# Gated delta-net on one core: the work behind each convolution is laid down 24 contraction tiles later, in steps of even period, with the output gates on their own and GpSimd taking scaling, masks and copies

## The chip, the core and the metric

One core of one Trainium2 chip runs the whole program. Its engines work side by side, each in the fixed order of its own queue: TensorE (PE in the profile, with its weight loads as PEld), VectorE (DVE), ScalarE (ACT), GpSimd (POOL) and the queue SP, which here issues the DMAs. The metric is the device time of one execution in microseconds; lower is better.

## What is computed

One inference step of a two-layer decoder trunk: a prompt of 512 tokens and 8 decoding sequences of 4 tokens each, 544 columns in all, width 1024. Layer 0 mixes tokens with an mLSTM, layer 1 with a gated delta-net; each is followed by a squared-ReLU MLP and layer norms. The change is in layer 1's mixer alone. Cut from the reference:

```python
proj = x @ w_in
qkv, z = proj[..., :CONV_DIM], proj[..., CONV_DIM:CONV_DIM + VW_B]
c = sum(xp[:, j:j + T] * conv_w[j] for j in range(4))      # xp: 3 old rows, then qkv
c = silu(c); new_conv = xp[:, T:]
q = l2norm(c[q part]) * DK_B ** -0.5; k = l2norm(c[k part]); v = c[v part]
# per head, in chunks: A = strictly lower part of (beta k) k^T * decay, plus I
u, w = triangular_solve(A, [beta v, beta k exp(G)])
for each chunk:
    v_new = u - w S
    o     = (q exp(G)) S + (q k^T * decay) v_new
    S     = exp(G_last) S + (k exp(G_last - G))^T v_new
o = head_rms(o) * norm_w * silu(z)
return o @ w_out, S, new_conv
```

There are 8 key heads and 16 value heads of 128 by 128. The prompt has one state per head, and each of the 8 decoding sequences has its own, which is read, used and written back.

## The kernel before

All large products are made of float32 values split into a high and a low part (`split`, L111 and L112: a copy on ACT, a subtraction on DVE), with three products for each contraction tile of 128: `mm3` (L194) issues them, 272 columns at a time, and calls `tick()` after each contraction tile. A "contraction tile" below is one such call, three matmuls. Weights come in blocks of 128 by 1024, by DMA into `wraw`, then split into `wh` (ACT) and `wl` (DVE).

Layer 1's mixer works on 8 units; a unit is one key head with its two value heads. The string `ORDER` sets the sequence of the large products: `p0` to `p7` project a unit (`project`: key, query and two values, 16 contraction tiles each), `y0` to `y3` project the output gates of a pair of units and apply them (`gate_out`), `w0` to `w3` multiply a pair with the output weights (`out`). Behind each of a unit's four projections stands `conv`: ACT copies the projection from PSUM into a padded buffer `pre`, ACT and DVE make the four-tap convolution `acc` (L996, L998), a sigmoid is made by a clamp on DVE (L510) and three ACT passes (L511 to L513), and DVE multiplies (L1002). Right behind it the code puts the transposes and norms that need its result (L1040, L1049, L1065).

The rest of a unit is cut into steps by `yield`, and three lanes run such steps: `lane_i` (`prepare` builds the decayed products and inverts 16 by 16 blocks on DVE, L1128 and L1130, sending them through DRAM, `dx`, back to `xc`; `invert` builds the full inverse with small matmuls L1167 to L1214), `lane_s` (`scan`: the chunk loop L1257, L1268, L1275, L1284, L1246), and `lane_d` (`decode` and `update` for the 8 sequences: L1371, L1422, and on DVE the masks L1414 and the states L1427). Every `tick()` counts a lane down, and at zero, every `period` contraction tiles, the lane runs its next step. `PERIODS` sets the periods for the lanes i, s and d: 3, 3, 4 from p0, 5, 5, 6 from y0, 3, 3, 6 from p7. Where a result must be there, `finish(...)` runs the steps of all lanes, one after another, with no contraction tile between them: in `gate_out` for the units of its pair, and before p3 to p7 for a unit whose buffers are wanted again. The inversion of eight units and these calls are the places that the prediction speaks of.

The place of an instruction in the code is its priority; when the program is built, each engine's queue is laid down in the order in which work is taken to be ready, so that neighbours in the code can change places. On the chip each queue is then worked off in that order, and an instruction that waits holds all behind it.

## Time and profile before

| | us |
|---|---|
| median of 3 runs | 1814.6 (1813.19 to 1815.72) |
| the profiled execution | 1814.86 |
| its span, first to last instruction | 1813.2 |
| TensorE busy | 1742.2 |
| VectorE busy | 1062.3 |
| ScalarE busy | 831.2 |
| GpSimd busy | 56.1 |
| the delta-net's stretch, from 705 to 1420 us of the span | 715 |

The span is the stretch that the rows below cover; the 1.7 us between it and the profiled execution's own time lie around it and stay as they are. "PEclk" in a row is the granted clock of TensorE as a share of 2.4 GHz; it has two levels, 1.0 (2.4 GHz) and 0.5 (1.2 GHz), and a value between them is a mean over the stretch.

### The profile page before, as it was taken

To read this page: it belongs to the slowest core of one execution; us is meant where nothing else is said; L and a number is where in the kernel's file an instruction comes from. 1 tells how busy PE (TensorE), PEld (TensorE's weight loads), DVE (VectorE), ACT (ScalarE), POOL (GpSimd) and SP (SyncE) were. 2 spreads that over 40 slices of the span, in tenths; PEclk is the share of its full clock that TensorE was granted. 3 is DMA by queue.
4 is the path that set the end of the run, shared out by engine and by line. 5 is a ranking of instruction groups with operands and counts; after the bars stand their busy time and mean duration, and the time that the engine had idled before them with its cause. 6 is when DMAs were issued, how large, how long until landed. Compare 5 with 4: busy or idle time off the path is not lost.

```text
span 1813.2 us, 35720 instructions
## 1 busy us (share of the span) xinstructions
PE 1742.2 (96%) x14580; PEld 1678.0 (93%) x14580; DVE 1062.3 (59%) x2648; ACT 831.2 (46%) x1874; POOL 56.1 (3%) x105
## 2 busy tenths in 40 slices
PE   7999999999999999899979999999898999999997
PEld 7999998999999999899869989998898999999996
DVE  6564767432244368777856877785488543234436
ACT  6444346331244137775644764575246542134314
POOL 2000000000000000011001000000000000000000
PEclk9999999999999999899979999997799999999998
DMA  4131232222223221223324323421242222222311
GB/s 161 59 106 62 70 97 93 71 94 82 94 82 117 82 75 62 56 58 102 104 64 143 105 66 104 141 80 39 78 132 73 94 85 91 90 86 93 106 59 50
DMA packets 84293, 158.89 MB, mean 88 GB/s; under 512 B 37536, under 2 KB 41504, under 8 KB 83616
## 3 DMA queue, kind: packets, MB, share of 16 engines
q1 hardware_dynamic: 84128, 156.60, 27.6%
q8 instruction: 115, 1.88, 0.4%
q14 instruction: 50, 0.41, 0.1%
HBM read 140.51 MB, written 16.06 MB: 86 GB/s over the span
## 4 chain that ended last, share of the span: by engine, by line
PE 80%; DVE 10%; ACT 4%; DMA 3%; issue 1%; POOL 1%; SPq 0%; ACTq 0%; DVEq 0%; POOLq 0%
PE pg_t L194 39%; PE pm_s L194 13%; PE pm_a L194 12%; PE pm_s L1371 2%; DVE lnt L380 1%; PE pm_s L1422 1%; DVE lnt L381 1%; PE pm_s L1257 1%; DMA xc<-dx 1%; PE pm_s L1268 1%; PE pm_a L1093 1%; DVE wl L112 1%; DVE acc L998 1%; PE pm_s L1275 1%; DVE XL L392 1%
## 5 line engine op out<-in xcount | busy, mean ns | idle before, releaser
L112 DVE TENSOR_TENSOR wl<-wraw,wh 128x1024 fp32r<-128x1024 f32 x200 | 245.3, 1227 | 370.6 <-ACT wh L111 369.8
L194 PE MATMUL pg_t<-XH,wh 128*128 128x272 f32 x1480 | 443.9, 300 | 3.3 <-ACT wh L111 2.8
L194 PE MATMUL pg_t<-XH,wl 128*128 128x272 f32 x1480 | 437.6, 296 | 1.0 <-DVE wl L112 1.0
L194 PE MATMUL pg_t<-XL,wh 128*128 128x272 f32 x1480 | 438.3, 296 | 0.0
L111 ACT CAST wh<-wraw 128x1024 fp32r<-128x1024 f32 (+1 forms) x201 | 210.1, 1045 | 472.7 <-PE pg_t L194 221.2
L194 PEld LDWEIGHTS pg_t<-XH,wh 128*128 128x128 f32 x1480 | 284.6, 192 | 7.4 <-ACT wh L111 4.5
L194 PEld LDWEIGHTS pg_t<-XH,wl 128*128 128x128 f32 x1480 | 283.8, 192 | 3.1 <-DVE wl L112 1.7
L194 PEld LDWEIGHTS pg_t<-XL,wh 128*128 128x128 f32 x1480 | 284.4, 192 | 2.0
L194 PE MATMUL pg_t<-h,wh 128*128 128x272 f32 x672 | 129.2, 289 | 0.0
L194 PEld LDWEIGHTS pg_t<-h,wh 128*128 128x128 f32 x672 | 105.8, 189 | 0.3
L194 PE MATMUL pg_t<-h,wl 128*128 128x272 f32 x336 | 97.0, 289 | 0.0
L194 PE MATMUL pm_a<-h,wh 128*128 128x272 f32 x496 | 95.3, 289 | 0.0
L194 PE MATMUL pm_s<-h,wh 128*128 128x272 f32 x496 | 95.0, 289 | 0.0
L194 PE MATMUL pm_s<-XH,wh 128*128 128x272 f32 x288 | 84.7, 294 | 0.0
L194 PE MATMUL pm_s<-XL,wh 128*128 128x272 f32 x288 | 84.4, 293 | 0.0
L194 PE MATMUL pm_s<-XH,wl 128*128 128x272 f32 x288 | 84.3, 293 | 0.0
L194 PE MATMUL pm_a<-XL,wh 128*128 128x272 f32 x280 | 82.3, 294 | 0.8 <-DVE XL L392 0.8
L396 DVE SCALAR_TENSOR_TENSOR XR<-XR,pg_t 128x272 f32<-128x272 f32 x118 | 51.0, 434 | 54.4 <-PE pg_t L194 53.9
L194 PE MATMUL pm_a<-XH,wh 128*128 128x272 f32 x280 | 82.6, 295 | 0.0
L194 PE MATMUL pm_a<-XH,wl 128*128 128x272 f32 x280 | 81.3, 290 | 0.0
L194 PEld LDWEIGHTS pm_s<-h,wh 128*128 128x128 f32 x496 | 78.0, 189 | 0.2
L194 PEld LDWEIGHTS pm_a<-h,wh 128*128 128x128 f32 x496 | 78.0, 188 | 0.1
(573 smaller groups left out, 3910.8 us busy)
## 6 DMA issues: line engine op xcount, KB each, us to landing
wraw<-in_w SPq DMA_DIRECT2D x64, 512.0 KB, 3.5
wraw<-in_wb SPq DMA_DIRECT2D x48, 512.0 KB, 3.5
wraw<-in_w2a SPq DMA_DIRECT2D x32, 512.0 KB, 3.5
sst<-in_s SPq DMA_DIRECT2D x64, 256.0 KB, 3.1
wraw<-in_wa SPq DMA_DIRECT2D x24, 512.0 KB, 3.5
wraw<-in_w2b SPq DMA_DIRECT2D x24, 512.0 KB, 3.5
wraw<-in_wbo SPq DMA_DIRECT2D x16, 512.0 KB, 3.7
out_ss<-sst SPq DMA_DIRECT2D x32, 256.0 KB, 2.7
```

The lines of the kernel that those rows point to most:

```text
L111: S.copy(hi, src)
L112: V.tensor_tensor(lo, src, r32(hi), op=ALU.subtract)
L194: T.matmul(ps, lhsT=wt[:, k, :], rhs=xt[k][:, HS[h]], start=first and k == 0 and q == 0, stop=last and k == n - 1 and q == 2,)
L380: V.tensor_tensor(t, x, rs, op=ALU.mult)
L381: V.tensor_tensor(t, t, mu, op=ALU.subtract)
L392: V.tensor_tensor(XL[j][:, HS[h]], x, r32(XH[j][:, HS[h]]), op=ALU.subtract)
L396: V.scalar_tensor_tensor(x, x, ALPHA if first else 1.0, ps, op0=ALU.mult, op1=ALU.add)
L998: V.scalar_tensor_tensor(acc, pre[:, q:q + WC], cw[q], acc, op0=ALU.mult, op1=ALU.add)
L1093: T.matmul(pk[:, q * 256:(q + 1) * 256], lhsT=kq[:, 0, c0:c0 + P], rhs=kq[:, :, c0:c0 + P], start=True, stop=True)
L1257: T.matmul(pks[:, w], lhsT=kq[:, w, cc], rhs=St, start=True, stop=True)
L1268: T.matmul(pv[:, j], lhsT=X[:, 4 * (ch // 2) + 2 * j + ch % 2], rhs=rhs[:, j] if ch else vtok[:, j, 0], start=True, stop=True)
L1371: T.matmul(pkq[:, r], lhsT=t[:, r], rhs=kqf[:, :, o:o + 4], start=True, stop=True)
```

## The change

- `ORDER` runs `g` in place of `y`, earlier: g0 follows p2, g1 follows p4, g2 follows p6, g3 stands between w2 and w3. `gate(g)` projects and makes the gates alone and keeps them in four `yh` buffers; `gated(u)`, a new step, multiplies them with a unit's outputs and splits the product. It runs in a fourth lane, `lane_m`.
- `finish` moves from the gates to the front of each `w`: w0 waits for `m1`, w1 for `m3`, w2 for `m5`, w3 for `m7`.
- `PERIODS` for i, s, d and m is 6, 5, 6, 4 from p0 on, and 4, 4, 6, 3 from w2 on.
- The transposes and norms behind a convolution become the functions `keys`, `queries` and `values`, put on the list `later`; `tick()` runs them 24 contraction tiles after (`LAG`). A unit's inversion then waits for its `q`, its scan for its `v`.
- In `prepare` the recursion on 16 by 16 blocks is one step, no longer five, and after the DMA of `xc` three empty steps follow (`REST`).
- GpSimd takes from DVE: in `conv` the clearing of `pre`, the copy of the old rows into it and the two copies to `cvo`; the copy in `kqx`; in `update` the masks `VM` (8 operations of 128 columns for 2 of 512), and the scaling of the states by their decay (4 of 128 columns). DVE's four multiply-adds of 128 columns for four states become one addition of 512 columns. `update` has three empty steps ahead of the first head of each half.
- The two products for the decoding tokens in `conv` become one.

The core of the diff:

```diff
-ORDER = "p0 p1 p2 p3 y0 w0 p4 p5 y1 w1 p6 p7 y2 w2 y3 w3"
-PERIODS = {"p0": (3, 3, 4), "y0": (5, 5, 6), "p7": (3, 3, 6)}
+ORDER = "p0 p1 p2 g0 p3 w0 p4 g1 p5 w1 p6 g2 p7 w2 g3 w3"
+PERIODS = {"p0": (6, 5, 6, 4), "w2": (4, 4, 6, 3)}
+LAG = 24
+REST = 3
...
+    def run_later():
+        key, work = later.pop(0)[1:]
+        work()
+        done.add(key)
 
     def tick():
+        now[0] += 1
+        while later and later[0][0] <= now[0]:
+            run_later()
         for lane in lanes:
             lane.tick()
...
-            V.memset(pre[:, 0:3], 0.0)
-            V.tensor_copy(samp(pre)[:, :, 0:3], cvt[:, slot])
+            G.memset(pre[:, 0:3], 0.0)
+            G.tensor_copy(samp(pre)[:, :, 0:3], cvt[:, slot])
...
-            V.tensor_copy(cvo[:, 0:3], pre[:, TP:TP + 3])
-            V.tensor_copy(cvo[:, 3:27].rearrange("p (b t) -> p b t", t=3), samp(pre)[:, :, 4:7])
+            G.tensor_copy(cvo[:, 0:3], pre[:, TP:TP + 3])
+            G.tensor_copy(cvo[:, 3:27].rearrange("p (b t) -> p b t", t=3), samp(pre)[:, :, 4:7])
...
+                later.append((now[0] + LAG, f"{'kq'[w]}{u}", (keys, queries)[w]))
...
-                if r % 3 == 0:
-                    yield
...
+            for _ in range(REST):
+                yield
...
-                    V.tensor_tensor(VM[w], vhl[:, w:w + 1].to_broadcast([P, 4, P]),
-                                    bmask[:, 4 * q:4 * q + 4].unsqueeze(2).to_broadcast([P, 4, P]), op=ALU.mult)
+                    for r in range(4):
+                        G.tensor_scalar(VM[w][:, r], vhl[:, w], bmask[:, 4 * q + r:4 * q + r + 1], None, op0=ALU.mult)
...
+                    for r in range(4):
+                        bb = NCH + 4 * q + r
+                        G.tensor_scalar(st[:, r], st[:, r], glc[:, bb:bb + 1], None, op0=ALU.mult)
+                    for _ in range(3 if h == 0 else 0):
+                        yield
...
-                        V.scalar_tensor_tensor(t, t, glc[:, NCH + bb:NCH + bb + 1], pS[:, r], op0=ALU.mult, op1=ALU.add)
+                    V.tensor_tensor(st, st, pS, op=ALU.add)
...
-                finish(f"s{2 * g + h // 2}", f"d{g}")
...
+        def gated(u):
...
+                V.tensor_tensor(t[:, :TP], sgm[:, :TP], units[u]["oT"][h - h0], op=ALU.mult)
+                V.tensor_tensor(t[:, TP:], sgm[:, TP:], ua["osm"][:, h * NS:(h + 1) * NS], op=ALU.mult)
...
+                split(yh[h], yl[h], t)
+                yield
...
+                finish(f"m{2 * i + 1}")
                 out(i, *units[2 * i]["y"])
```

Three places of the queues show what moved. The first is TensorE where the inversion of unit 6 begins (`DT`, `DB`, `Z`, `U`: parts of the blocks; `acc` or `vtokb`: the values behind a convolution; `XH`, `XL`: the parts of the layer's input). Before:

```order
L194 MATMUL pg_t<-XH_82,wl 128x272
L1065 MATMUL pm_t<-ident,acc 128x128 x4
L1167 MATMUL pm_a<-DT,U 32x16 x32
L194 MATMUL pg_t<-XH_75,wh 128x272
L1174 MATMUL pm_a<-DB,Z 32x16 x32
L194 MATMUL pg_t<-XL_83,wh 128x272
```

and now:

```order
L206 MATMUL pg_t<-XH_75,wl 128x272
L1186 MATMUL pm_a<-DT,U 32x16 x32
L206 MATMUL pg_t<-XH_76,wh 128x272
L206 MATMUL pg_t<-XL_84,wh 128x272
L206 MATMUL pg_t<-XH_76,wl 128x272
L206 MATMUL pg_t<-XH_77,wh 128x272
L1193 MATMUL pm_a<-DB,Z 32x16 x32
```

The transposes of the values no longer stand right ahead of the inversion, there are 72 matmuls of contraction tiles ahead of it, and 4 instead of 1 between its first two products.

The second place is TensorE around the last matmul of the last gate's projection, where w3 begins (`gyh`, `gyl`, `wx`: w3's own operands; `go_on`, `St`, `rhs`, `vd`, `vn`: the scan of unit 7; `tok`, `UAs`, `onx`: the end of the last `decode`). Before:

```order
L194 MATMUL pg_t<-XL_90,wh 128x272
L194 MATMUL pg_t<-XH_82,wl 128x272
L194 MATMUL pg_t<-gyh,wh 128x272
...
L194 MATMUL pm_a<-gyh,wx 128x272
L1246 MATMUL pm_s<-ident,go_on 128x128 x2
L194 MATMUL pm_s<-gyh,wx 128x272
```

and now:

```order
L1265 MATMUL pm_s<-ident,go_on 128x128 x2
L1276 MATMUL pm_s<-St,kq 128x256 x2
L206 MATMUL pg_t<-XH_82,wl 128x272
L1405 MATMUL pm_s<-tok,sx 128x128
L1287 MATMUL pm_s<-rhs,X 128x128 x2
L1294 MATMUL pm_s<-vd,ktok 128x256
L1413 MATMUL pm_s<-sx,UAs 128x128
L1303 MATMUL pm_s<-vn,A 128x128 x2
L1419 MATMUL pm_s<-ident,onx 128x128
L1265 MATMUL pm_s<-ident,go_on 128x128 x2
L1276 MATMUL pm_s<-St,kq 128x256 x2
L206 MATMUL pm_a<-gyh,wh 128x272
```

Before, one transpose of the scan was left when the gates' last matmul was over; now its last two chunks and the end of the last `decode` are, and behind what is shown stand 30 matmuls of w3 and then 12 of `update`.

The third place is GpSimd around the inversion of unit 1. Before:

```order
L1151 MEMSET X 128x1024
L1153 TENSOR_SCALAR DB<-xc,par 128x8x16 x2
L1179 COPY X<-DB 32x8x32 x4
L1180 COPY ZX<-DT 32x8x32
```

and now:

```order
L1440 TENSOR_SCALAR sst<-sst,glc 128x128 x8
L1172 TENSOR_SCALAR DB<-xc,par 128x8x16 x2
L1434 TENSOR_SCALAR VM<-vhl,bmask 128x128 x8
L997 MEMSET pre 128x3
L998 COPY pre<-cvt 128x8x3
L1198 COPY X<-DB 32x8x32 x4
L1199 COPY ZX<-DT 32x8x32
```

States, masks and the preparation of a convolution's buffer now stand in one queue with the inversion's copies.

## Rows read from the trace of the kernel before

**Rows 1.** Busy time by stretch: start:end, length, engines' busy, granted clock, DMA share, GB/s.

```profile
705.00:765.00 60.00, 53.22 (x364) 51.34 (x363) 47.39 (x140) 44.00 (x109) 0.95 (x1) 0.89 0.19 51
...
835.00:895.00 60.00, 58.34 (x600) 54.07 (x599) 44.41 (x139) 39.23 (x104) 6.74 (x9) 0.94 0.32 93
895.00:935.00 40.00, 28.55 (x329) 23.75 (x328) 20.99 (x73) 14.20 (x38) 3.54 (x8) 0.70 0.33 106
935.00:1065.00 130.00, 129.59 (x1171) 122.85 (x1170) 101.37 (x327) 75.60 (x210) 5.49 (x10) 1.00 0.36 106
1065.00:1085.00 20.00, 16.76 (x309) 14.84 (x308) 11.95 (x33) 11.17 (x21) 4.44 (x8) 0.91 0.23 61
...
1225.00:1255.00 30.00, 27.32 (x339) 24.36 (x337) 13.66 (x33) 13.60 (x30) 3.80 (x8) 0.66 0.15 41
...
1275.00:1315.00 40.00, 34.94 (x395) 31.45 (x394) 17.38 (x58) 9.75 (x26) 3.77 (x8) 0.74 0.29 86
...
1365.00:1420.00 55.00, 49.46 (x353) 46.10 (x353) 46.80 (x117) 36.91 (x78) 0.00 (x0) 1.00 0.23 76
705.00:1420.00 715.00, 675.92 (x6298) 632.56 (x6297) 527.98 (x1600) 414.86 (x1064) 41.53 (x71) 0.94 0.30 89
```

**Rows 2.** TensorE's waits from 705 to 1420 us: line, for whom, total, times, longest.

```profile
PE pm_a L1167 <- DVE DT L1159: 5.6, 3, 4.3
PE pm_t L1065 <- DVE acc L1002: 5.0, 3, 2.8
PE pm_t L1040 <- DVE kq L1002: 3.3, 1, 3.3
PE pm_s L1246 <- DVE xb L1130: 3.1, 1, 3.1
PE pm_a L1093 <- DVE kq L1002: 2.1, 1, 2.1
```

**Rows 3.** Chain of waits, in order of time: contraction matmuls that follow each other.

```profile
1038.70 5.79 PE pg_t L194 x46
```

**Rows 4.** TensorE in order of time: the three products of one step of an update.

```profile
904.80 0.86 PE L1422 MATMUL pm_s<-VM,KM 128*128 128x512 f32 x3
```

**Rows 5.** The last chunk of unit 7's scan and its gating, in order of time.

```profile
1365.57 1.03 PE L1257 MATMUL pm_s<-St,kq 128*128 128x256 f32 x4
...
1369.00 0.61 PE L1284 MATMUL pm_s<-vn,A 128*128 128x128 f32 x4
1374.66 0.41 PE L1246 MATMUL pm_s<-ident,go_on 128*128 128x128 f32 x2 [1.92 <-DVE go_on L1233]
...
1376.86 1.49 DVE L112 TENSOR_TENSOR gyl<-sgmz,gyh 128x544 fp32r<-128x544 f32 x2
```

**Rows 6.** VectorE's groups from 705 to 1420 us: count, busy, mean ns, idle before.

```profile
L1427 DVE SCALAR_TENSOR_TENSOR sst<-sst,glc,pm_s 128x128 f32<-128x128 f32 x128 | 37.1, 342 | 9.5 <-PE pm_s L1422 9.0 <-DMA out_ss<-sst 0.4
L1414 DVE TENSOR_TENSOR VM<-vhl,bmask 128x512 fp32r<-128x512 f32 x16 | 10.7, 682 | 0.9 <-PE pm_s L1422 0.8
L992 DVE COPY cvo<-pre 128x24 f32<-128x24 f32 x32 | 5.8, 182 | 0.9 <-ACT pre L989 0.9
L986 DVE COPY pre<-cvt 128x24 f32<-128x24 f32 x32 | 5.7, 178 | 0.2 <-issue 0.2
L991 DVE COPY cvo<-pre 128x3 f32<-128x3 f32 x32 | 5.1, 159 | 0.0
L985 DVE MEMSET pre<- 128x3 f32 x32 | 2.0, 61 | 0.0
```

**Rows 7.** GpSimd's operations on `DB`: count, shortest, median and longest in ns.

```profile
L1179 POOL COPY X<-DB x32: 387/396/1297, 785.6 to 1305.0; 32x256 f32<-32x256 f32 x32
L1153 POOL TENSOR_SCALAR DB<-xc,par x16: 597/602/890, 780.6 to 1295.9; 128x128 f32<-128x128 f32 x16
```

**Rows 8.** GpSimd and VectorE side by side in order of time.

```profile
1075.88 2.60 POOL L1179 COPY X<-DB 32x256 f32<-32x256 f32 x4 [3.09 <-DVE DB L1176]
...
1076.85 1.36 DVE L112 TENSOR_TENSOR wl<-wraw,wh 128x1024 fp32r<-128x1024 f32 x1 [0.17 <-ACT wh L111]
```

More of the change, by code (lines that the diff above doesn't have):

```diff
@@ L158, in tick @@
                 self.step()
-    lanes, done = [], set()
+    lanes, done, later, now = [], set(), [], [0]
+    def run_later():
+        key, work = later.pop(0)[1:]
+        work()
+        done.add(key)
     def tick():
+        now[0] += 1
+        while later and later[0][0] <= now[0]:
+            run_later()
         for lane in lanes:
@@ L168, in finish @@
         while not done.issuperset(keys):
+            if later:
+                run_later()
             for lane in lanes:
@@ L1031, in project, with transposed, keys, queries @@
             j0 = 2 * (u % 2)
+            scl = gp.tile([P, 3, NCH, 2], F32, tag="scl", name="scl", bufs=3)
+            cols2 = lambda o: colp[:, :, HV * o + 2 * u:HV * o + 2 * u + 2]
+            wide = lambda t: t.unsqueeze(2).to_broadcast([P, NCH, 2])
+            def transposed(src):
+                pt = mtile("t")
+                for ch in range(NCH):
+                    T.transpose(pt[:, ch * P:(ch + 1) * P], src[:, ch * P:(ch + 1) * P], ident)
+                return pt.rearrange("p (c d) -> p c d", c=NCH)
+            def keys():
+                S.copy(ktok, transposed(kq[:, 0]))
+                for ch in range(NCH):
+                    sq = gp.tile([P, P], BF16, tag="k_sq", name="k_sq", bufs=1)
+                    S.activation(sq, ktok[:, ch], AF.Square, accum_out=lnk[:, ch:ch + 1])
+                S.activation(lnk, lnk, AF.Ln, bias=eps_rms)
+            def queries():
+                pt = mtile("t")
+                for ch in range(NCH):
+                    T.matmul(pt[:, ch:ch + 1], lhsT=flat[1][:, ch * P:(ch + 1) * P], rhs=ones[:, 0:1], start=True, stop=True)
+                S.activation(lnq, pt[:, 0:NCH], AF.Ln, bias=eps_rms)
+                S.activation(nrm[:, 1, 0], lnk, AF.Exp, scale=0.5)
+                S.activation(nrm[:, 2, 0], lnk, AF.Exp, scale=-1.0)
+                V.tensor_tensor(scl[:, 0], cols2(0), wide(lnk), op=ALU.subtract)
+                V.tensor_tensor(scl[:, 1], cols2(1), wide(nrm[:, 1, 0]), op=ALU.mult)
+                V.tensor_tensor(scl[:, 2], cols2(3), wide(nrm[:, 2, 0]), op=ALU.mult)
+                q_scales(nrm[:, 1, 1], nrm[:, 2, 1], lnq)
+            def values(j):
+                V.tensor_tensor(vtok[:, j], transposed(flat[j]), scl[:, 1, :, j:j + 1].to_broadcast([P, NCH, P]), op=ALU.mult)
+            flat = [vtok[:, j].rearrange("p c d -> p (c d)") for j in range(2)]
             for w in range(2):
@@ L1069, in project @@
+                conv(ct + 2 + j, cvt, 2 + j, flat[j], vsx[:, j0 + j].rearrange("p (b t) -> p b t", t=TS), pss)
+                later.append((now[0] + LAG, f"v{u}" if j else f"v{u}_", lambda j=j: values(j)))
             st.update(nrm=nrm, scl=scl, kq=kq, ktok=ktok, vtok=vtok, kqx=kqx, vsx=vsx)
@@ L1472, in after @@
             yield from steps
-        lane_i, lane_s, lane_d = lanes[:] = [Lane() for _ in range(3)]
+        lane_i, lane_s, lane_d, lane_m = lanes[:] = [Lane() for _ in range(4)]
         for w in ORDER.split():
@@ L1482, in hybrid_kernel @@
                     finish(f"s{i - NKQ}")
-                units.append(project(i))
-                lane_i.add(f"i{i}", unit(i))
-                lane_s.add(f"s{i}", after({f"i{i}"} | ({f"w{(i - 3) // 2}"} if i % 2 and i > 2 else set()), scan(units[i])))
+                units.append({})
+                units[i].update(project(i))
+                lane_i.add(f"i{i}", after({f"q{i}"}, unit(i)))
+                lane_s.add(f"s{i}", after({f"i{i}", f"v{i}"} | ({f"w{(i - 3) // 2}"} if i % 2 and i > 2 else set()), scan(units[i])))
+                lane_m.add(f"m{i}", after({f"s{i}", f"d{i // 2}", f"g{i // 2}"}, gated(i)))
                 if i % 2:
@@ L1489, in hybrid_kernel @@
                     lane_d.add(f"u{i // 2}", after({f"i{i}"}, update(*pair)))
-            elif what == "y":
-                gate_out(i)
+            elif what == "g":
+                gate(i)
             else:
+                finish(f"m{2 * i + 1}")
                 out(i, *units[2 * i]["y"])
```

73 lines of the change are left out of this document (21 added, 52 removed).

## The prediction

> **What bounds the kernel now.** TensorE: by the profile's table it is busy for 1742.2 of 1813.2 us. The change touches only the stretch from 705 to 1420 us, so I read that stretch in pieces [rows 1]. A busy TensorE can still lose time there, since at a granted clock of 0.5 (1.2 GHz) a busy microsecond does half the work. So for each piece I take its length less TensorE's busy time, plus (1 - PEclk) times the busy time. Over the whole stretch that is 39.1 + 0.06 x 675.9 = 79.7 us: no rearrangement of this stretch can win more, because both programs issue the same matmuls. It lies in seven places:
>
> - 705 to 765, first convolutions: 6.8 + 0.11 x 53.2 = 12.6
> - 835 to 895: 1.7 + 0.06 x 58.3 = 5.2
> - 895 to 935, the steps that gate y0 calls for, then an inversion: 11.4 + 0.30 x 28.6 = 20.0
> - 1065 to 1085: 3.2 + 0.09 x 16.8 = 4.7
> - 1225 to 1255, inversion of unit 6: 2.7 + 0.34 x 27.3 = 12.0
> - 1275 to 1315, the steps that y2 calls for: 5.1 + 0.26 x 34.9 = 14.1
> - 1365 to 1420, end of the mixer and its layer norm: 5.5
>
> Together 74.1; the other 5.6 is spread thin, and 935 to 1065 shows how little a well-covered piece loses: 0.4 us in 130. Next come TensorE's waits [rows 2]. The longest are for the blocks' inverse (4.3 us in one piece), for a value or key behind its convolution (5.0 and 3.3 us) and for the recursion `xb` (3.1 us). All are waits for a chain of small work on DVE and ACT which the queue put too near to its source. They are short; the clock then costs as much again: from 1225 to 1255 us only 2.7 us are idle, but the clock stays at 0.5 through the inversion's small matmuls, and that takes 9.3.
>
> **The change, part by part.** I cost each place as what it will lose afterwards.
>
> *Lag, periods and empty steps in mid-stretch.* At 1065 and 1225 the waits are for the values behind a convolution. Now the transposes of unit 6's values are away from the inversion, 72 contraction matmuls lie ahead of it, and each product has 4 to 8 behind it. One takes 5.79 / 46 = 0.126 us [rows 3], so 9 us stand where waits of 2.8 us and less were; the three empty steps, 18 contraction tiles or 6.8 us, cover the DMA's way to `xc`. Next late there is the sequence Z, ZX between the small products, which 4 to 8 matmuls hide as they do from 935 to 1065. I leave 1 us at 1065 and 1.5 at 1225. From 835 to 895 it was `finish` before p3; by my count of steps unit 0's scan (16 steps of period 5 behind 15 of period 6, 170 contraction tiles) is over when p3 comes (192 tiles), so 1.5 stays. From 1275 to 1315 y2's `finish` goes altogether, since w2 comes long after unit 5's scan: 1.5 stays.
>
> *Start.* The 12.6 are two waits, 2.1 and 3.3 us, each followed by a low clock. The transposes of unit 1's keys stand behind the same contraction matmul in both queues, so the lag moves nothing there. What shrinks is the chain: each convolution loses the DVE's clearing and three copies, 61 + 178 + 159 + 182 ns [rows 6], 0.58 us, and five convolutions stand ahead, 2.9 us against a wait of 3.3. The second wait may go, the first not. Between 3 and 12.6 I take 7.
>
> *w0.* `finish("m1")` stands where y0's `finish` stood, two products later, and little is left then: the last step of unit 1's scan and the gating. But its chain is bare. A chunk from `St` to its transposes takes 1374.66 - 1365.57 = 9.1 us, of which 5.0 lie behind `vn`, and from there to the last split part it is 1376.86 + 1.49 - 1374.66 = 3.7 us [rows 5]. Against these 8.7 us stand 21 contraction matmuls (2.6) and six update products (2 x 0.86 [rows 4]), with more waits in the inversion of unit 2 that runs along: idle about 8, and the low clock through that inversion 7 (it took 8.6 and 9.3 in the pieces above). 15 of the 20.0 stay; bounds 7 and 20.
>
> *End.* This gets worse. Before, a single transpose of unit 7's scan was left when the gates' last matmul was over, and the place loses 5.5. Now two chunks are left, and the end of the last `decode`: 2 x 9.1 + 3.7 = 21.9 us. Cover: 31 contraction matmuls (3.9), twelve update products (4 x 0.86 = 3.4) and some 2 us of the scan's own matmuls (an estimate: `St` and `vn` of rows 5, once more for the other chunk): 12.6 idle. Then w3 stands behind the second half's masks, which GpSimd makes only when the first half's are used up: 8 x 0.602 = 4.8 [rows 7], less 15 contraction matmuls (1.9): 2.9. Low clock on some 9 us of work: 4. The layer norm's own waits: 2.5. In all 22; bounds 10 and 34.
>
> *The moves to GpSimd.* DVE is busy 528 of 715 us and TensorE is not behind it in general, so what DVE gains is worth only what the places above say. It loses 37.1 + 10.7 + 18.6 us [rows 6] and gets 32 additions of 512 columns, at the masks' 0.682 us 21.8: 528 becomes about 483. GpSimd gets 64 masks and 128 scalings of 128 columns at 0.602 [rows 7], 116 us, and small copies at DVE's prices, 19: 41.5 becomes some 180 of 690. What hides that is GpSimd's idle time. But a GpSimd copy of 396 ns took up to 1297 [rows 7], and one group of four took 2.60 us where 4 x 0.396 is 1.6, beside a split of a weight block on DVE [rows 8]. Even with 1297 / 396 = 3.3 times everywhere GpSimd would be busy 500 us, not the bound. A gain of its own is excluded, as TensorE's waits for DVE are already counted above; a loss can only come through a wait, and that is rival 1. I take 0 in the sum.
>
> The Trainium skill, SBUF — State Buffer, section "Who interferes with whom", says that the port pair which VectorE and GpSimd share is an exclusive lock held for a whole instruction, and that the loser is fully blocked. This case's rows agree with it (396 against 1297 ns), and it speaks against the change: by it each of the 192 large operations can stand behind one split, which makes rival 1 likelier than the busy time does.
>
> **Sum.** 7 + 1.5 + 15 + 1 + 1.5 + 1.5 + 22 = 49.5 where 74.1 stood: 24.6 us less. 1814.9 - 24.6 = 1790.3 us. The profiled execution, 1814.86, lies 0.3 above the median, so 1790.
>
> **Rivals.**
>
> 1. *GpSimd's queue holds the convolutions: slower, 1828.* In the new queue 11 of 32 clearings of `pre` stand behind four or more scalings or masks, and those wait for state DMAs. ACT's first pass over `pre` waits for the clearing, and ACT's casts of weights wait behind it, so TensorE would run dry. Four operations are 2.4 us at 0.602 and 5.2 at 1.3; with 3.5, 11 x 3.5 = 38 us, 1790 + 38 = 1828. It decides from 24.6 / 11 = 2.2 us per place. Against it: a weight block is split one product ahead, 48 matmuls or 6 us, and the buffers are cleared early. Chance 0.12.
> 2. *The waits only move: no change, 1813.* If w0 costs what y0 did (20), the start stays (12.6), and the end costs y0's and y2's together (34), 12.6 + 1.5 + 20 + 1 + 1.5 + 1.5 + 34 = 72.1 stay. For it: the lanes' work has to be done by w3, and at longer periods more is left. Chance 0.10.
> 3. *The lag does little:* the queue puts the transposes where it takes them to be ready, whatever the code says, as for unit 1's keys. Then 1065 keeps 4.7 and the start 12.6: 1790 + 3.7 + 5.6 = 1799. Chance 0.08.
> 4. *The bare chains are shorter:* without weight casts between them, start 3, w0 7, end 10: 24.6 + 4 + 8 + 12 = 48.6 us less, 1766. Chance 0.20.
>
> **How the numbers follow.** My forecast, 1790, has 0.50. The range runs from rival 4 to rival 2, 1766 to 1813, which are also the sums of the bounds at start, w0 and end; outside stays rival 1 and little of the rest. About 0.2% (3.6 us) is what a measurement of this kernel can tell from no change. Faster: 0.50 + 0.20 + 0.08 = 0.78; same 0.10; slower 0.12.
>
> **What would show it.** In the pieces of time afterwards: no wait over 1 us on the inversions of units 3 to 7, and a clock of 1.0 around them; the waits for values gone; a dip of the clock and 5 to 10 us of idle TensorE at the front of w0; the largest loss, over 15 us, in the last 40 us before the layer norm, with waits for `go_on` and for masks; GpSimd busy 180 to 250 us in the whole span. The prediction is wrong in its mechanism if TensorE waits for `wh` or `wl` behind a GpSimd wait, or if the inversions still run at 0.5; it is wrong in size if the end is under 10 us.

## The result, and the profile after

The changed kernel takes 1834.4 us (median; 1820.3 to 1850.7), 1.0075 times the kernel before (95% interval 1.0050 to 1.0099), where 1790 had been predicted. It is slower, by less than 1%, and outside the range. Of its 20 executions one took 9386 us and is left out of these bounds, and the profiled one, 1849.5 us with a span of 1847.8, is among the two slowest of the others, 1.6% above the fastest. The median of the kernel before was 1819.9 us this time, while its profiled execution took 1814.9: the two profiles differ by 34.7 us, the medians by 14.6. So the rows below show where the change loses, and more of the loss than a median execution has. Its other executions differ from the profiled one by their granted clock, which runs from 0.973 at 1820 us to 0.955 at 1851.

First the engines' busy time over the whole span, then the pieces of the delta-net's stretch (columns as in [rows 1]):

```profile
PE 1768.0 (96%) x14580; PEld 1699.3 (92%) x14580; DVE 1031.7 (56%) x2360; ACT 824.9 (45%) x1874; POOL 221.2 (12%) x441
```

```profile
core 0: us, PE busy (x) PEld busy (x) DVE busy (x) ACT busy (x) POOL busy (x), PEclk, DMA share, GB/s
705.00:765.00 60.00, 55.62 (x414) 53.31 (x413) 47.00 (x102) 48.65 (x122) 11.24 (x37) 0.97 0.22 59
...
845.00:880.00 35.00, 32.58 (x391) 28.75 (x391) 19.39 (x47) 20.61 (x57) 12.50 (x26) 0.85 0.17 47
...
905.00:940.00 35.00, 28.79 (x346) 25.11 (x347) 19.82 (x50) 16.05 (x45) 6.07 (x15) 0.71 0.30 86
...
1060.00:1095.00 35.00, 30.85 (x359) 28.38 (x358) 13.30 (x25) 16.07 (x38) 7.49 (x18) 0.66 0.23 65
...
1155.00:1185.00 30.00, 27.08 (x339) 24.81 (x338) 10.79 (x24) 13.00 (x34) 11.82 (x26) 0.66 0.15 46
...
1245.00:1275.00 30.00, 27.43 (x339) 24.84 (x337) 13.23 (x26) 13.86 (x34) 5.20 (x16) 0.66 0.17 48
...
1333.00:1370.00 37.00, 34.97 (x376) 32.35 (x375) 12.08 (x23) 13.28 (x29) 9.26 (x16) 0.63 0.20 55
1370.00:1425.00 55.00, 45.07 (x262) 39.86 (x262) 33.79 (x84) 23.59 (x65) 24.77 (x40) 0.84 0.37 116
```

TensorE runs the same 14580 matmuls as before but is busy 1768.0 - 1742.2 = 25.8 us longer; its mean granted clock is 0.956, where it was 0.971. It stands idle 79.8 us of the span instead of 71.0, 8.8 more. By the prediction's measure, idle plus (1 - PEclk) times busy, the four pieces from 1060 to 1370 lose 14.6, 12.1, 11.9 and 15.0 us, 53.6 together. They are the inversions of units 4, 5, 6 and 7. Of TensorE's waits from 690 to 1460 us three rows tell why:

```profile
PE pm_a L1186 <- DVE DT L1178: 13.1, 7, 4.2
PE pm_s L1265 <- DVE go_on L1252: 5.1, 6, 1.4
PE pm_s L1447 <- POOL VM L1434: 2.8, 1, 2.8
```

L1186 is the first product of an inversion (L1167 in [rows 2], 5.6 us there). At units 4 to 7 it waits 4.15, 2.92, 2.57 and 2.03 us, and behind these waits the clock is at 0.5 for 23.5, 20.5, 20.5 and 27.3 us. The waits for values and keys of [rows 2] have left the list's head, as forecast.

The way to that product at unit 5, in three timelines (start, duration, instruction, count; in brackets the idle time ahead and what ended it). SyncE's queue:

```profile
1146.29 0.46 SPq L1150 DMA_DIRECT2D dx<-xb  x1
1148.58 3.48 SPq L1316 DMA_DIRECT2D sst<-in_s  x2
1152.16 0.39 SPq L1152 DMA_DIRECT2D xc<-dx  x1
```

GpSimd:

```profile
1149.13 2.35 POOL L1440 TENSOR_SCALAR sst<-sst,glc 128x128 f32<-128x128 f32 x4 [25.96 <-DMA sst<-in_s]
1151.64 3.23 POOL L1440 TENSOR_SCALAR sst<-sst,glc 128x128 f32<-128x128 f32 x4 [0.17 <-issue]
...
1156.11 2.34 POOL L1440 TENSOR_SCALAR sst<-sst,glc 128x128 f32<-128x128 f32 x4
1158.44 1.18 POOL L1172 TENSOR_SCALAR DB<-xc,par 128x128 f32<-128x128 f32 x2
```

VectorE and TensorE behind it:

```profile
1159.65 0.45 DVE L1178 STREAM_TRANSPOSE DT<-DB 128x256 f32<-128x256 f32 x1 [3.57 <-POOL DB L1172]
```

```profile
1156.94 0.29 PE L206 MATMUL pg_t<-XH,wl 128*128 128x272 f32 x1
1160.15 0.88 PE L1186 MATMUL pm_a<-DT,U 32*32 32x16 f32 x64 [2.92 <-DVE DT L1178]
```

The recursion ends at 1145.8. Its result is stored (`dx`), loaded again (`xc`), masked on GpSimd (`DB`, two operations that stood on GpSimd before the change as well) and transposed; 14.4 us pass to the product. The store lands 4.2 us after its issue, at about 1150.4; the load is issued 1.7 us later, behind a state load in SyncE's queue, and lands 3.5 us after that, at about 1155.7. The masks begin at 1158.44, 2.7 us later, when four more scalings of the state are done.

At units 4, 6 and 7 GpSimd held nothing: the masks begin 0.1 to 0.2 us after `xc` has landed. There the store is the longer part. SyncE's queue at unit 4, first before the change, then after:

```profile
1065.19 0.47 SPq L1133 DMA_DIRECT2D dx<-xb  x1
1068.00 0.38 SPq L1135 DMA_DIRECT2D xc<-dx  x1
```

```profile
1058.81 0.47 SPq L1150 DMA_DIRECT2D dx<-xb  x1
1063.43 0.32 SPq L1316 DMA_DIRECT2D sst<-in_s  x1
1063.85 0.39 SPq L1152 DMA_DIRECT2D xc<-dx  x1
```

From the store's issue to the load's it takes 5.0, 5.9, 4.4 and 4.2 us at units 4 to 7, where it took 2.8, 2.5, 1.9 and 2.2 before.

### The profile page after: what moved, and what is told of

It is laid out like the page before. It is cut to its first block, busy times and chain, and to the rows that moved or that the text cites. A ratio compares the mean times of both kernels' runs of the same rounds, so it can differ in the third digit from the quotient of the medians.

```text
span 1847.8 us, 35828 instructions
## 1 busy us (share of the span) xinstructions
PE 1768.0 (96%) x14580; PEld 1699.3 (92%) x14580; DVE 1031.7 (56%) x2360; ACT 824.9 (45%) x1874; POOL 221.2 (12%) x441
## 3 DMA queue, kind: packets, MB, share of 16 engines
q1 hardware_dynamic: 84128, 156.60, 27.3%
## 4 chain that ended last, share of the span: by engine, by line
PE 42%; DVE 5%; POOL 2%; DMA 2%; ACT 1%; issue 1%; SPq 0%; ACTq 0%; POOLq 0%; DVEq 0%
PE pg_t L206 20%; PE pm_s L206 6%; PE pm_a L206 6%; POOL sst L1440 1%; PE pm_s L1390 1%; PE pm_s L1276 1%; PE pm_s L1287 1%; PE pm_s L1447 1%; PE pm_s L1294 1%; PE pm_a L1233 1%; PE pm_a L1227 1%; PE pm_a L1112 1%; PE pm_s L1303 1%; DMA dx<-xb 1%; DMA xc<-dx 1%
## 5 line engine op out<-in xcount | busy, mean ns | idle before, releaser
L206 PE MATMUL pg_t<-XH,wh 128*128 128x272 f32 x1480 | 449.5, 304 | 6.1 <-ACT wh L113 4.7
L206 PE MATMUL pg_t<-XH,wl 128*128 128x272 f32 x1480 | 443.3, 300 | 1.0 <-DVE wl L114 1.0
L206 PE MATMUL pg_t<-XL,wh 128*128 128x272 f32 x1480 | 443.2, 300 | 0.0
L206 PEld LDWEIGHTS pg_t<-XH,wh 128*128 128x128 f32 x1480 | 288.7, 195 | 11.3 <-ACT wh L113 6.4
L206 PEld LDWEIGHTS pg_t<-XH,wl 128*128 128x128 f32 x1480 | 288.3, 195 | 3.1 <-DVE wl L114 1.8
L206 PEld LDWEIGHTS pg_t<-XL,wh 128*128 128x128 f32 x1480 | 288.8, 195 | 2.5
L1440 POOL TENSOR_SCALAR sst<-sst,glc 128x128 f32<-128x128 f32 x128 | 89.7, 717 | 111.5 <-DMA sst<-in_s 102.9
L1011 DVE SCALAR_TENSOR_TENSOR acc<-pre,cst,acc 128x568 f32<-128x568 f32 x96 | 77.1, 807 | 15.7 <-ACT acc L1009 10.7
```

The lines of the kernel that those rows point to most:

```text
L206: T.matmul(ps, lhsT=wt[:, k, :], rhs=xt[k][:, HS[h]], start=first and k == 0 and q == 0, stop=last and k == n - 1 and q == 2,)
L1011: V.scalar_tensor_tensor(acc, pre[:, q:q + WC], cw[q], acc, op0=ALU.mult, op1=ALU.add)
L1440: G.tensor_scalar(st[:, r], st[:, r], glc[:, bb:bb + 1], None, op0=ALU.mult)
```

## The experiments

Sixteen kernels. The table gives the ratio to the kernel before on the same chip, and from each kernel's one profile the waits of the inversions' first product (total us, times, from 690 to 1460 us), TensorE's busy time and its mean granted clock. The profile is of a single execution, and executions of one kernel differ by up to 1.8%, so small differences in the last three columns say little.

| run | edit | ratio (95%) | waits | busy | clock |
|---|---|---|---|---|---|
| before | | 1 | 6.4, 4 | 1742.2 | 0.971 |
| after | | 1.0075 (1.0050 to 1.0099) | 13.1, 7 | 1768.0 | 0.956 |
| e1 | after, 10 empty steps | 0.9979 (0.9955 to 1.0004) | 3.9, 2 | 1736.1 | 0.978 |
| e2 | after, recursion cut again | 0.9925 (0.9897 to 0.9953) | 7.5, 3 | 1734.9 | 0.979 |
| e3 | after, no moves to GpSimd | 1.0011 (0.9980 to 1.0042) | 8.2, 7 | 1744.4 | 0.973 |
| e4 | after, lag 0 | 1.0012 (0.9971 to 1.0052) | 13.0, 6 | 1756.9 | 0.964 |
| e5 | after, scalings and VM on DVE | 0.9929 (0.9895 to 0.9963) | 7.4, 7 | 1726.8 | 0.984 |
| e6 | after, masks DB on DVE | 0.9942 (0.9912 to 0.9971) | 6.1, 4 | 1736.2 | 0.976 |
| e7 | e2 and e3 | 0.9979 (0.9951 to 1.0007) | 3.1, 4 | 1728.0 | 0.981 |
| e8 | after, xc by ScalarE's queue | 1.0144 (1.0085 to 1.0203) | 13.3, 8 | 1752.6 | 0.965 |
| e9 | e5 and e6 | 0.9829 (0.9803 to 0.9856) | 2.7, 3 | 1720.6 | 0.987 |
| e10 | before, scalings and VM on GpSimd | 1.0001 (0.9972 to 1.0030) | 12.8, 5 | 1751.0 | 0.965 |
| e11 | e5, lag 0 | 1.0030 (1.0000 to 1.0061) | 9.1, 7 | 1741.4 | 0.974 |
| e12 | e9, 8 empty steps | 0.9864 (0.9835 to 0.9892) | none | 1729.8 | 0.980 |
| e13 | e9, convolutions' copies on DVE | 0.9882 (0.9853 to 0.9911) | 1.6, 3 | 1728.8 | 0.981 |
| e14 | e9, recursion cut again | 0.9888 (0.9851 to 0.9925) | none | 1726.5 | 0.983 |
| e15 | before, masks DB on DVE | 0.9955 (0.9932 to 0.9978) | 4.4, 2 | 1732.1 | 0.978 |
| e16 | before, recursion in one go, 3 empty steps | 1.0038 (1.0006 to 1.0071) | 3.3, 4 | 1765.2 | 0.958 |

**e1: is it the wait?**

```diff
-REST = 3
+REST = 10
```

> Ten empty steps instead of three between the recursion and the inversion; nothing else changes. In TensorE's queue the first product of the inversion then stands 120 to 150 contraction matmuls (15 to 19 us) later for units 4 to 6 and 45 (5.7 us) later for unit 7. Theory A (the product stands 2 to 4 us too near to the way of the recursion's result through DRAM, and the wait is what sends the clock to 0.5 for the rest of the inversion): the product's waits of 4.15, 2.92, 2.57 and 2.03 us at units 4 to 7 go, the clock there is 1.0, 20 to 27 us of half clock per inversion go: about 4 x 14 = 56 us less than the profiled run of after, 45 less than its median, minus 5 to 10 given back at the end since the scans start later: 1790 (1778 to 1805). Theory B (the inversion's small products, spread thin between contraction matmuls, lower the clock by themselves, wait or no wait): the waits go, the 0.5 stays: 1824 (1815 to 1835). Theory C (GpSimd's queue holds the masks of the inversion): no change at unit 5, little elsewhere, 1830.

Measured: the products of units 4, 5 and 6 wait for nothing, and the clock is at 1.0 for the 35 us behind each. Pieces around units 4 to 7:

```profile
1088.00:1125.00 37.00, 36.79 (x484) 35.00 (x484) 21.59 (x57) 13.69 (x35) 3.71 (x7) 1.00 0.32 99
1170.00:1205.00 35.00, 34.13 (x455) 32.12 (x456) 22.31 (x48) 19.60 (x43) 4.17 (x10) 1.00 0.20 63
1255.00:1290.00 35.00, 34.66 (x445) 32.36 (x446) 23.47 (x62) 14.63 (x36) 3.36 (x6) 0.95 0.15 45
1322.00:1360.00 38.00, 31.60 (x389) 27.79 (x387) 19.99 (x45) 20.32 (x53) 12.24 (x20) 0.87 0.24 77
```

Theory A holds where the wait went, theory B falls: the same spread products run at full clock. The 0.95 of the third row is a dip that ends ahead of the inversion; unit 7 still waits 2.8 us and still dips; there the masks stood 3.1 us behind scalings on GpSimd. The time, 1818, missed its range (one of its ten executions took 2786 us and is left out). A part of what is missing shows in the profile: at the start, from 705 to 765 us, 5.8 + 0.13 x 54.2 = 12.9 us are lost, where the change lost 6.1, and at w0 it is 10.5 + 0.26 x 29.5 = 18.2 us, where the change lost 14.6:

```profile
890.00:930.00 40.00, 29.50 (x236) 22.05 (x235) 28.31 (x88) 15.87 (x50) 16.66 (x29) 0.74 0.44 129
```

**e2: the recursion cut again.**

```diff
                 V.tensor_tensor(xb[:, 0:r, r:16], xb[:, 0:r, r:16], tv, op=ALU.subtract)
+                if r % 3 == 0:
+                    yield
```

> The recursion is cut into its five steps again as before the change, the three empty steps stay. In TensorE's queue the first product then stands 32, 12 and 1 contraction matmuls later for units 4 to 6, and 30 earlier for unit 7. Theory A: the wait of 4.15 us at unit 4 shrinks by 4 us, unit 5's 2.92 by 1.5, units 6 and 7 keep theirs; one or two of four paced inversions run at full clock: 15 to 25 us less, 1815 (1805 to 1830). Theory B: no change, 1834. Theory C: no change, 1834.

Measured: no wait at units 4 and 5, as A has it for unit 4, 1.30 us at unit 6, 2.77 at unit 7 with 27 us at half clock, and a wait of 3.41 at unit 3, where the masks began 4.1 us after the load had landed, behind GpSimd's `VM`. Faster than expected, 1806.

**e3: everything back on VectorE.** The edits in `conv` and `kqx` (the lines stand for five), and those of e5 below:

```diff
-            G.memset(pre[:, 0:3], 0.0)
+            V.memset(pre[:, 0:3], 0.0)
```

> All work that the change gave to GpSimd is back on VectorE in the form it had before (the state is scaled and added in one instruction again, one instruction makes a mask); everything else is as after the change. The first products keep their places in TensorE's queue to within 30 contraction matmuls. Theory A: the chain behind the recursion loses only GpSimd's own delay (about 2 to 4 us at unit 5, where the masks of the inversion stand behind eight scalings, under 1 us elsewhere), so unit 5's wait goes and the other three stay: 1825 (1815 to 1838). Theory C (GpSimd is the loss): 1834 less 35 to 45, near 1795. A third case: VectorE's extra 66 us delay the recursions, the waits grow, 1845.

Measured: 1821 us, which is within theory A's range, but the waits are not A's: 1.62, 0, 1.12 and 1.15 us at units 4 to 7, each smaller, not unit 5's alone. So the moves to GpSimd are not the whole loss, and they touch more than one inversion.

**e4: lag 0.**

```diff
-LAG = 24
+LAG = 0
```

> The work behind the convolutions is laid down with no lag (0 tiles instead of 24), everything else as after the change. The first products keep their places to within 30 contraction matmuls, so under theory A their four waits and the low clock stay, and the waits for keys and values behind their convolution come back (before the change 5.0 and 3.3 us, and 4.7 to 9 us at half clock beside): 1842 (1830 to 1855). If the lag itself did the harm (it lets the inversion and the transposes fall together): 1815. If the queue places the transposes where it takes them to be ready whatever the code says, no change: 1834 within 5.

Measured 1.0012, no loss, and if anything a gain on the change, since the two intervals barely meet; the first products' waits are the same (13.0 us), and waits for keys and values do not return to the head of the list. Here the third reading was nearest, but see e11.

**e5 and e6: which of GpSimd's work?** e5 gives the scalings and the masks `VM` back to VectorE:

```diff
-                    for r in range(4):
-                        G.tensor_scalar(VM[w][:, r], vhl[:, w], bmask[:, 4 * q + r:4 * q + r + 1], None, op0=ALU.mult)
+                    V.tensor_tensor(VM[w], vhl[:, w:w + 1].to_broadcast([P, 4, P]),
+                                    bmask[:, 4 * q:4 * q + 4].unsqueeze(2).to_broadcast([P, 4, P]), op=ALU.mult)
...
-                        G.tensor_scalar(st[:, r], st[:, r], glc[:, bb:bb + 1], None, op0=ALU.mult)
...
-                    V.tensor_tensor(st, st, pS, op=ALU.add)
+                    for r in range(4):
+                        bb = NCH + 4 * q + r
+                        V.scalar_tensor_tensor(st[:, r], st[:, r], glc[:, bb:bb + 1], pS[:, r], op0=ALU.mult, op1=ALU.add)
```

e6 only moves the two masks of the inversion, which the change had not touched:

```diff
-                G.tensor_scalar(DB[:, :, 16 * q:16 * q + 16], xc, par[:, q:q + 1], None, op0=ALU.mult)
+                V.tensor_scalar(DB[:, :, 16 * q:16 * q + 16], xc, par[:, q:q + 1], None, op0=ALU.mult)
```

> Of the work given to GpSimd only the scaling of the state and the masks of the decode's values go back to VectorE, in the form of before; the clearing and the copies of the convolutions stay on GpSimd. Theory D (the state's scalings lengthen the way of the recursion's result: the load of the recursion's result stands in SyncE's queue behind a state load that waits for a buffer, 4.15 us at unit 4 and 3.5 at unit 5, and the inversion's masks stand behind scalings on GpSimd, 4 us at unit 5): as with everything back on VectorE, first-product waits of 1.6, 0.1, 1.1 and 1.2 us at units 4 to 7, ratio to before 1.001 (0.998 to 1.004), against 1.0075 for the whole change. If the convolutions' clearing and copies were the harm: waits as in the whole change, 1.0075.

> The two masks of the inversion (from the recursion's result to DB), which were on GpSimd before the change already, are on VectorE; all else as after the change. Theory D: unit 5's wait of 2.92 us goes, since there the masks stood behind eight scalings; at unit 4, 6 and 7 the result itself comes late, so the waits lose only the masks' own difference (1.2 us on GpSimd): 4.15 to about 3, 2.57 to 1.4, 2.03 to 1. Ratio to before 1.002 (0.997 to 1.006). If GpSimd's place in the chain doesn't matter: waits unchanged, 1.0075. If VectorE's own queue delays the masks by as much: no change or more.

Measured: 0.9929 and 0.9942, both better than expected. In e5 the products of units 4 to 7 wait 0.19, 0, 2.18 and 1.98 us, and from the store's issue to the load's it takes 1.9, 2.0, 3.4 and 4.0 us. So at units 4 and 5 that part of the way became shorter too. Theory D puts it down to the state load ahead in SyncE's queue (see e8); what shortens the store itself is not shown. e3 differs from e5 only by the convolutions' five lines and is 0.8% slower (1.0011 against 0.9929): the copies and clearings are better off on GpSimd, the scalings and masks are not.

The edit of e6, sixteen instructions in all, is worth 1.0075 - 0.9942 = 1.3%, some 24 us. Unit 5 there, on VectorE's timeline:

```profile
1134.00 0.19 DVE L1392 COPY kqs<-pm_s 128x32 f32<-128x32 f32 x1 [2.96 <-PE pm_s L1390]
1134.11 0.47 DVE L1172 TENSOR_SCALAR DB<-xc,par 128x128 f32<-128x128 f32 x2
1134.62 0.45 DVE L1178 STREAM_TRANSPOSE DT<-DB 128x256 f32<-128x256 f32 x1
```

From the recursion's end to the product it is 8.8 us instead of 14.4, and the product doesn't wait. At unit 4 it still waits 2.52 us, in this execution with no half clock behind it, and at unit 6 it waits 1.61 us with 20.5 us of half clock. That GpSimd is part of the way is shown.

**e7: the edits of e2 and e3 together.**

> Both together: the recursion in five steps, and everything that was given to GpSimd back on VectorE. Cut alone gave 0.9925 of before, VectorE alone 1.0011, the whole change 1.0075. If they cure different waits they add: 0.9925 - 0.0064 = 0.986, 1798. If they cure the same waits (the same four inversions), there is nothing left for the second: 0.9925, 1810. If GpSimd's help with VectorE's load is what made the cut version good: 0.997, 1818.

Measured 0.9979: they don't add, and the sum is worse than e2. The third reading fits: the convolutions' copies are back on VectorE here, and e13 shows a loss of the same size from them alone.

**e8: the load by another queue.**

```diff
-            dma(xc, dx.rearrange("s b i j -> (b i) s j"))
+            nc.scalar.dma_start(xc, dx.rearrange("s b i j -> (b i) s j"))
```

> Only the load of the recursion's result is issued from ScalarE's queue instead of SyncE's; all else as after the change. Theory D: at unit 4 it no longer stands behind the state load (4.15 us in SyncE's queue) but starts when the store has landed, about 2 us sooner: the wait of 4.15 falls to about 2; unit 5's falls only if GpSimd's queue gives way, to 1 to 3; units 6 and 7, where the store itself took 4 us, stay at 2 to 2.6. One or two inversions run at full clock: ratio 1.002 (0.996 to 1.007). Rival: ScalarE waits in its queue for the store (2 to 4 us, eight times) and the casts of weights behind it come late: TensorE waits for wh, ratio 1.012.

Measured 1.0144. At unit 4 the load was issued 4.49 us behind the store (1063.70 against 1059.21), hardly sooner than by SyncE (5.04): the store itself took that long, and the state load ahead of `xc` in SyncE's queue was not what held it there. That half of theory D falls at unit 4; at unit 5 of the change the state load did hold it, for 1.7 us. The rival's sign, TensorE waiting for `wh`, is not there: 1.4 us, as in the change. The ratio comes from four executions and its interval overlaps the change's, so whether the version is slower than the change, its waits being about the same 13.3 us, stays open.

**e9: the edits of e5 and e6 together.**

> The state's scalings and the decode's masks back on VectorE, and the inversion's two masks DB on VectorE too; the rest as after the change. Theory D (the way from the recursion to the first product is too long for the place that the queue gives the product, and GpSimd is part of that way): the masks take 0.5 us instead of 1.2 and wait for nothing on GpSimd, so the waits left with the scalings alone undone (1.58, 2.18 and 1.98 us at units 2, 6 and 7) fall by 0.5 to 1 us; one more inversion at full clock, 5 to 10 us less: ratio to before 0.989 (0.985 to 0.994), against 0.9929 and 0.9942 for the two alone. If both cure the same waits: 0.993. If VectorE's queue now delays the masks: 0.997.

Measured 0.9829, 1793.2 us (1791.3 to 1795.2): the fastest, faster than both kernels, and more than either reading gave. Its pieces at the start, w0, the inversions of units 4 to 7 and the end:

```profile
705.00:765.00 60.00, 56.14 (x407) 53.84 (x407) 46.76 (x103) 46.76 (x120) 11.49 (x38) 0.94 0.22 61
885.00:925.00 40.00, 32.06 (x395) 26.86 (x394) 29.35 (x98) 21.20 (x58) 7.75 (x15) 0.91 0.32 95
1050.00:1080.00 30.00, 29.58 (x423) 27.70 (x423) 20.41 (x45) 20.60 (x58) 7.03 (x17) 1.00 0.21 58
1125.00:1155.00 30.00, 30.00 (x428) 27.99 (x426) 19.22 (x48) 21.45 (x63) 7.01 (x20) 1.00 0.24 68
1212.00:1240.00 28.00, 27.05 (x401) 25.07 (x400) 19.01 (x43) 22.79 (x63) 6.93 (x18) 1.00 0.18 50
1288.00:1318.00 30.00, 28.88 (x409) 26.96 (x409) 15.17 (x33) 14.44 (x31) 2.33 (x6) 0.94 0.34 101
1318.00:1395.00 77.00, 63.61 (x396) 55.73 (x395) 62.48 (x171) 46.19 (x110) 0.00 (x0) 0.93 0.27 88
```

By the same measure: 7.2, 10.8, 0.4, 0, 0.9, 2.9 and 17.8. The inversions lose 4.2 us where the profiled execution of the change loses 53.6, and the end is the largest piece that is left.

**e10 and e16: one part of the change in the kernel before.** e10 brings in the lines that e5 takes out. e16:

```diff
-                if r % 3 == 0:
-                    yield
...
+            for _ in range(3):
+                yield
```

> The kernel before the change, with one part of the change alone: the state's scalings and the decode's masks on GpSimd in the form of the change. If GpSimd's scalings stand in the way of the inversion's masks whatever else is changed: the first products' waits of 0.1 to 0.8 us at units 0, 4, 5 and 6 grow to 1 to 4 us, more half clock, ratio to before 1.008 (1.003 to 1.015). If they do harm only with the recursion in one go and the new periods (where they fall on the masks by chance): 1.000 (0.997 to 1.003). If VectorE's relief is what counts in the old order: 0.995.

> The kernel before the change, with one part of the change alone: the recursion in one go and three empty steps behind its load. The first products stand within 30 contraction matmuls of where they stood, since the queue puts them where it takes them to be ready. If the recursion in one go brings the waits of 2 to 4 us by itself: waits of 1 to 3 us at most units, 1.006 (1.002 to 1.012). If the cut was of no matter there: 1.000 (0.997 to 1.003). If the recursion in one go is faster (13 to 15 us instead of 14 to 18) and nothing else counts: 0.997.

e10: no difference in time, though in its profile the inversion's masks of units 2, 3 and 7 stand behind scalings and one product waits 9.1 us, in steps that y0 calls for. So the harm does not come "whatever else is changed". e16: slower by 0.4%, as expected, but not by the wait that was named: the first products' waits stay small (3.3 us in all). From its list of TensorE's waits:

```profile
PE pm_t L1065 <- DVE acc L1002: 5.5, 3, 3.7
PE pm_s L1246 <- DVE tb L1128: 4.6, 2, 2.4
...
PE pm_a L1167 <- DVE DT L1159: 2.6, 3, 1.4
```

`tb` and `xb` are the recursion itself: TensorE's waits put down to it are 8.4 us in all, where they were 5.6 before. Whether that makes the 0.4% is not shown; the longest stretches of half clock in this profile are behind the first products of units 1 and 4, which waited 0.94 and 0.28 us.

**e11: the lag in the mended kernel.** e5 with e4's edit.

> As the version with the scalings and the decode's masks back on VectorE (0.9929), but with the lag of the work behind the convolutions at 0 tiles instead of 24. If the queue puts the transposes where it takes them to be ready whatever the code says: the same places within a few matmuls, 0.993 (0.990 to 0.997). If the lag is what removed the waits for keys and values (5.0 and 3.3 us and the half clock behind them): 1.000 (0.997 to 1.004).

Measured 1.0030 against 0.9929: here, with e5's edit, the lag is worth 1%, though not by the waits for keys and values that it was meant to end. What grows without it are the first products' waits, 9.1 us for e5's 7.4, and unit 0's, 2.29 us, has 22 us at half clock behind it; in TensorE's queue that product stands 50 contraction matmuls earlier without the lag. In the change as it stands (e4) the lag shows no such gain.

**e12 and e14: more distance in the mended kernel.** e9 with `REST = 8`, and e9 with e2's edit.

> As the version with the scalings, the decode's masks and the inversion's masks on VectorE, and with eight empty steps between the recursion and the inversion instead of three. In TensorE's queue the first product then stands where the code lays it down, 20 to 50 contraction matmuls later at units 2 to 5, but 30 earlier at units 6 and 7. Theory D: the waits of units 2 to 5 go, those of units 6 and 7 stay or grow to 2 to 4 us: 0.991 (0.986 to 0.998). If a product that is far from its source is all that counts: 0.986. If the scans, which start later, give it back at the last output projections, as with ten steps: 0.997.

> As the version with scalings, decode's masks and inversion's masks on VectorE (0.9829), with the recursion in five steps again. If the recursion in one go is itself a part of the harm: first-product waits at 0 for units 0 to 6, 0.978 (0.975 to 0.982). If the step only matters by where it leaves the first product, and the shorter way has already cured that: 0.983 (0.980 to 0.986). If the later scans cost at the end: 0.988.

Measured 0.9864 and 0.9888: no first product waits at all, and both are slower than e9. Their pieces at w0 (890 to 930 us), e12 first:

```profile
890.00:930.00 40.00, 28.94 (x288) 21.27 (x289) 28.08 (x106) 13.98 (x46) 3.90 (x9) 0.66 0.41 116
```

```profile
890.00:930.00 40.00, 28.95 (x309) 21.39 (x309) 29.73 (x111) 15.30 (x49) 3.90 (x9) 0.74 0.40 116
```

They lose 20.9 and 18.6 us where e9 loses 10.8: a likely reason, not tested by itself, is that a scan that begins later has more left when w0 calls for it. So the recursion in one go is no harm where the way behind it is short.

**e13 and e15: the rest of GpSimd's work, and the masks alone.** e13 is e9 with the five lines of e3's edit; e15 is the kernel before with e6's edit.

> As the version with scalings, decode's masks and inversion's masks on VectorE (0.9829), and the convolutions' clearing and copies back on VectorE too, so that nothing is left of the moves to GpSimd. If the copies on GpSimd pay (VectorE is on the way to the first product: everything on VectorE gave 1.0011 where the scalings alone gave 0.9929): 0.991 (0.986 to 0.996), with first-product waits of 1 us and more at units 0 and 2. If they are worth nothing, as the prediction put it: 0.983 within 0.003.

> The kernel before the change, with the inversion's two masks on VectorE instead of GpSimd, nothing else. If the way to the first product was a cost in the kernel before as well (waits of 0.76, 0.55 and 0.71 us at units 0, 5 and 6, and half clock of 19.4 us at unit 6): 0.996 (0.993 to 1.000). If its losses are the waits for values and the steps called for by the gates alone: 1.000.

e13: 0.9882 against 0.9829; the convolutions' small work on GpSimd is worth about 0.5%, but not by the first products, which wait less here (1.6 us) than in e9 (2.7). Much of it is at w0, where 10.9 + 0.23 x 34.1 = 18.7 us are lost and 10.8 in e9; why is not shown:

```profile
885.00:930.00 45.00, 34.09 (x393) 30.27 (x392) 32.67 (x112) 21.41 (x53) 4.94 (x7) 0.77 0.33 98
```

e15: the kernel before gains 0.45% by the masks alone, so a part of e9's gain was to be had without the change. In its profile, which is of its fastest execution, the wait of unit 6 falls from 0.71 to 0.22 us and the half clock behind it from 19.4 to 3.4 us.

## Why the prediction was wrong

- **Start, w0, end: near in size.** Forecast 7, 15 and 22; measured 4.4 + 0.03 x 55.6 = 6.1, 6.2 + 0.29 x 28.8 = 14.6, and 9.9 + 0.16 x 45.1 = 17.1 to 1425 us with 2.9 idle behind it. w3's wait for masks (2.9 forecast) is there with 2.8 (L1447). At the start the forecast let one of the two waits for keys stay, and both went. Where y2's steps stood, 1.7 us are lost from 1275 to 1333 (1.5 forecast), and the waits for values became short.
- **Inversions: the step that failed.** "9 us stand where waits of 2.8 us and less were; the three empty steps, 18 contraction tiles or 6.8 us, cover the DMA's way to `xc`", and a clock of 1.0 at units 3 to 7. Forecast some 2.5 us in all, measured 53.6 at units 4 to 7 and 2.4 + 0.15 x 32.6 = 7.3 at unit 1 where 1.5 was forecast. With these sizes, and 6 us less for start, w0 and end, the sum is 1790 + 51 + 6 - 6 = 1841 us. The profiled execution took 1849.5 and the median 1834.4: this step holds the miss, and the profile gives it a larger size than the median has.
- Three errors are in that step.
- (a) The empty steps are a distance in the code. In TensorE's queue the product had already left the place where the code put it: at units 4 to 7 some 100 to 150 contraction matmuls stand ahead of it that the code lays down behind it, since the queue has it where it takes its operands to be ready. By that count three empty steps (54 matmuls) decide nothing; seven more (126) do (e1). The prediction knew this of the transposes (its third rival) and didn't apply it here.
- (b) "The DMA's way to `xc`" is only a part, and it was too long: from the recursion's end to the product it takes 9.9, 14.4, 8.5 and 8.4 us at units 4 to 7, and at unit 7 this is store, load, masks and transpose with almost nothing in between. TensorE had work for 5.8, 11.5, 6.0 and 6.3 us of that, and stood for the rest. "72 contraction matmuls lie ahead of it" says nothing of this, as long as it isn't counted from the recursion's end.
- (c) **The moves to GpSimd were taken as 0.** They are two terms of opposite sign. Scalings and masks `VM` cost: undone (e5), the change goes from 1.0075 to 0.9929. The convolutions' copies gain: undone as well (e3), it is 1.0011. The first rival asked who on GpSimd's queue waits behind the scalings and looked at the convolutions alone; the third place of the change's queues, ahead of the prediction, shows the other customer, `DB`. It was held behind them for 2.7 us at unit 5, and for 4.1 and 3.1 us in e2 and e1, but not at units 4, 6 and 7 of the change, where the longer store made the way long.
- No one of these is the cause alone. Putting the product later (e1, e2), the scalings back (e5) or the masks elsewhere (e6) each takes 1.0 to 1.5% off, and together they give less than the sum (e7, e9); in the kernel before, the scalings (e10) did no harm. What they have in common is the way from the recursion to the product, set against TensorE's work in between.
- **The rule on the shared port** (the Trainium skill, SBUF — State Buffer, "Who interferes with whom"): the trace agrees as far as it shows a delay; whether the loser was blocked or slowed it does not tell. Four scalings took 2.35 and 2.34 us, and 3.23 where VectorE split a weight block beside them; the mean over all 128 is 717 ns, where the masks `DB` of as many elements took 602 in [rows 7]. At unit 5 the order of GpSimd's queue weighed more than the slower operations: 2.7 us of standing behind others against 0.115 us for each; 0.115 us x 128 is 15 us of an engine that is 12% busy.
- **First rival:** the right engine with the wrong victim; its price of 1828 is near the median by chance. Second: not what happened, as the old places did get better. Third: that the lag does little fits e4, but its price doesn't, as the start fell to 6.1. Fourth: no, as w0 and the end cost 14.6 and 17.1 where it had 7 and 10.
- The other terms stand nearly by themselves in e9, where the scalings and `VM` stay on VectorE and `DB` is moved to it. Its ratio is 0.9829; the sum had forecast 1790 / 1814.9 = 0.986 for the whole change. That they are so near is in part luck: `DB` on VectorE, which the forecast did not have, is worth 0.45% in the kernel before (e15).

What is not settled: what made the store longer; why the lag's gain shows in e5 and not in the change; what makes e16 slower, and whether e8 is; and which waits the clock answers (below).

## What to carry to other kernels

When work is given to an idle engine, list everybody who already has instructions there and ask of each how long it can wait: a short operation on the critical way stood 2.7 us behind four others at one inversion, and moving two operations of 0.6 us for each unit to another engine brought 1.3%. A distance written into the code is worth nothing unless the queue that is built from it keeps it: look where the consumer stands against its source, add up the source's whole way, and count a wait ahead of a stretch of small matmuls as several times its length: with waits of 2.0 to 4.2 us the four pieces lost 11.9 to 15.0 us each, as the clock was at half behind them.
